# Two-layer hybrid decoder: the conditioning's slabs in the MLPs move from the weights' load places to the place of the dead normed tokens

## The chip, the cores and the metric

The kernel runs on one core of one Trainium2 chip. The metric is device time of one execution in microseconds (us). The engines are PE (TensorE, with its weight loads shown apart as PEld), DVE (VectorE), ACT (ScalarE), POOL (GpSimd) and SP (SyncE, which here only issues transfers). "The trace" is the hardware profiler's record of one execution of the kernel before.

## What is computed

Two layers of a trunk over 256 tokens of width 1024. Each layer has a part with four token mixers and an MLP. A vector c is turned by `ada_w` into six vectors per layer, the conditioning: shift, scale and gate for the mixers, and the same for the MLP.

```
c_act = silu(c)
for l in range(2):
    sh1, sc1, g1, sh2, sc2, g2 = split(c_act @ ada_w[l] + ada_b[l], 6)
    h = rmsnorm(x, norm_mix_g[l]) * (1 + sc1) + sh1
    z = h @ w_in[l]                        # 7124 columns, for the four mixers and their gates
    ... four mixers, merged by gates ...
    x = x + g1 * (merged @ w_o[l])
    h = rmsnorm(x, norm_mlp_g[l]) * (1 + sc2) + sh2
    x = x + g2 * (square(relu(h @ mlp_w1[l])) @ mlp_w2[l])
out = rmsnorm(x, final_g)
```

All of it is float32. The matrix products are made of three products of float32r parts: each weight is split into a high and a low part, and so are the tokens.

## The kernel before

**Slabs.** Every weight reaches the core as slabs of 128 partitions x 1024 float32 (512 KB; those of `w_in` may be smaller). SP loads a slab into a place named `raw`; there are five of these (`NB_RAW = 5`, pool `rawp`). ACT copies it to the high part `wh`, DVE subtracts to make the low part `wl`, and after that the place is free for the next load. `wh` and `wl` have nine places in the MLPs. PE then multiplies with both.

**The conditioning on DVE.** Ten of the twelve conditioning vectors are made on DVE (`ON_DVE`): eight slabs each of the transposed `ada_w` (`in_ada_t`). For one slab DVE multiplies it with the broadcast c (`crow`) and adds up the row, in one SCALAR_TENSOR_TENSOR that writes back into the slab's own place (`Vec.use`); nothing of it goes to ACT or PE. Those slabs sit in the same five `raw` places as the weights and are freed by that instruction. Two vectors are made at the kernel's start in places of their own (`raw0`). `PLAN` puts one in the first mixers, six in the first layer's MLP (48 slabs) and one in the second layer's MLP (8 slabs).

**The MLP.** The 4096 hidden columns are taken in 16 groups g of 256. W1 of a group is two slabs, W2 of a group two slabs. PE does W1 of groups 0 to 2 for one token half at a time, then W2 of groups 0 and 1, and from then on in turns W1(g), W2(g-1) up to W1(13), W2(12), then W1(14), W1(15), and then the rest of W2. What I call a phase below is two slabs, W1 or W2 of one group. After W1(g) ACT and POOL make the squared relu, DVE its low part `uL`, which W2(g) needs. `spread` strews the conditioning's items evenly among the items from W2(0) on.

**What sets the order.** The program is written out in one order for each engine's queue by `run()`: it walks through the items, and before an item it calls `do_split` for the slabs that the item and the next ones need (about 5500 ns ahead by the planner's own clock `Flow`), and `do_load` for the next slabs as long as a place is free in its books (`raw_free`). A load stands in SP's queue in the order of the slabs, and waits there until its place is free: SP goes on to no later load before. Likewise a SCALAR_TENSOR_TENSOR on DVE waits for its slab and holds up the `wl` behind it.

**The normed tokens.** `new_hT` makes two tiles of 128 x 8 x 256 (tags `hTh` and `hTl`, 8 KB a partition each, one buffer each, pool `actp`) for the normed tokens of the mixers. In the MLP they are dead: the MLP has its own `h2`. At the end of the first MLP they are made anew for the second layer's mixers.

Of the kernel before, what the change touches and what calls it, by code (L numbers as in the profile page):

```python
# [23 lines left out]
F32 = mybir.dt.float32  # L24
# [5 lines left out]
OP = mybir.AluOpType  # L30
# [3 lines left out]
P = 128  # L34
S = 256
NT = 2
D = 1024
KD = 8
# [21 lines left out]
PLAN = {('start', 0): ((0, 1), (0, 0)), ('mixers', 0): ((0, 3), (0, 4), (0, 2)), ('mlp', 0): ((0, 5), (1, 1), (1, 0), (1, 3), (1, 4), (1, 2)), ('mixers', 1): (), ('mlp', 1): ((1, 5),)}  # L60
ON_PE = ((0, 3), (0, 4))
ON_DVE = tuple((l, p) for l in range(2) for p in range(6) if (l, p) not in ON_PE)
# [240 lines left out]
class Slab:  # L303


    pre = use = None
    first = False

    def __init__(self, ap, shape, split=True):
        self.ap, self.shape, self.split = ap, shape, split  # L310
# [14 lines left out]
def trunk_kernel(ctx, tc, x, cT, pos, chan, ada_w, ada_t, w_in, mlp_w1, gla_gate_w,  # L325
                 gla_norm_g, hgrn_norm_g, w_branch_out, w_o, mlp_w2, final_g, out, depth=2):
    nc = tc.nc
    fl = Flow(nc)
    V, A, G, T = fl.v, fl.a, fl.g, fl.t
# [3 lines left out]
    rawp = ctx.enter_context(tc.tile_pool(name="rawp", bufs=NB_RAW))  # L333
    hlp = ctx.enter_context(tc.tile_pool(name="hlp", bufs=NB_HL))
    rows = ctx.enter_context(tc.tile_pool(name="rows", bufs=1))
    actp = ctx.enter_context(tc.tile_pool(name="actp", bufs=1))
# [41 lines left out]
    slabs = []  # L378
    pos_of = {"load": 0, "split": 0}
# [3 lines left out]
    def add(emit, need=(), before=None, cost=1300.0):  # L383
        items.append(Item(emit, need, before, cost))
        return items[-1]

    def spread(start, fill):

        main = items[start:]
        del items[start:]  # L390
        n = 0
        for i, it in enumerate(main):
            while n < len(fill) and n * len(main) < i * len(fill):
                items.append(fill[n])
                n += 1
            items.append(it)
        items.extend(fill[n:])
# [10 lines left out]
    def view(t_, shape):  # L408
        n = 1
        for d in shape[1:]:  # L410
            n *= d
        v = t_[:, :n]
        return v.rearrange("p (a b) -> p a b", b=shape[2]) if len(shape) == 3 else v

    raw_free = [0.0] * NB_RAW
    raw0 = {"free": [0.0] * NB_RAW0}
    hl_free = {"hl": [0.0] * NB_HL, "hl2": [0.0] * NB_HL2}
    sp = {"t": 0.0}

    def do_load(i):  # L420
        s = slabs[i]
        if s.pre is not None:
            s.pre()
        s.raw = view((raw0["pool"] if s.first else rawp).tile([P, 1024], F32, name="raw", tag="raw"), s.shape)
        nc.sync.dma_start(s.raw.rearrange("p a b -> p (a b)") if len(s.shape) == 3 else s.raw, s.ap)
        n = 1
        for d in s.shape:
            n *= d
        places = raw0["free"] if s.first else raw_free
        free = places.pop(0) + 60.0 if len(places) else 0.0  # L430
        sp["t"] = max(sp["t"], free) + 475.0
        start = max(fl.clock["dma"], sp["t"] + 650.0)
        fl.clock["dma"] = start + n * 4 / 360.0
        s.t_raw = fl.clock["dma"] + 908.0
        fl.arrived(s.raw, s.t_raw)

    def do_split(i, pool):
        s = slabs[i]
        if s.use is not None:
            old, fl.ctx = fl.ctx, None  # L440
            s.use()
            (raw0["free"] if s.first else raw_free).append(fl.clock["dve"])
            fl.ctx = old
        if not s.split:
            return
        s.pool = pool
        live_hl[pool] += 1
        pl = hlp if pool == "hl" else hl2["pool"]
        free = hl_free[pool].pop(hl_free[pool].index(min(hl_free[pool])))
        wh = pl.tile([P, 1024], F32R, name="wh", tag="wh")  # L450
        wl = pl.tile([P, 1024], F32R, name="wl", tag="wl")
        fl.freed(wh, free)
        fl.freed(wl, free)
        s.h, s.l = view(wh, s.shape), view(wl, s.shape)
        old, fl.ctx = fl.ctx, None
        A.activation(s.h, s.raw, AF.Copy)
        V.tensor_tensor(s.l, s.raw, s.h.bitcast(F32), op=OP.subtract)
        raw_free.append(fl.end)
        fl.ctx = old

    def run():
        order = {}
        last = {}
        for j, it in enumerate(items):
            for s in it.need:
                if id(s) not in order:
                    order[id(s)] = len(slabs)
                    slabs.append(s)
                last[id(s)] = j
        n = len(items)  # L470
        closing = [n] * (n + 1)
        for j in range(n - 1, -1, -1):
            closing[j] = j if items[j].closes else closing[j + 1]

        def room(s, j):
            go = ["hl"] if live_hl["hl"] < NB_HL else []
            if hl2["pool"] is not None and live_hl["hl2"] < NB_HL2 and last[id(s)] < closing[j]:
                go.append("hl2")
            return min(go, key=lambda p: min(hl_free[p])) if go else None

        for j, it in enumerate(items):
            if it.before is not None:
                it.before()
            must = max([order[id(s)] for s in it.need], default=-1)
            want, t, k = must, 0.0, j
            while k + 1 < n and t < (LOOK if it.look is None else it.look):
                k += 1
                want = max([want] + [order[id(s)] for s in items[k].need])
                t += items[k].cost
            while pos_of["split"] <= want:  # L490
                i = pos_of["split"]
                pool = room(slabs[i], j) if slabs[i].split else "none"
                if pool is None:
                    assert i > must, "no room for a slab"
                    break
                while pos_of["load"] < len(slabs) and (pos_of["load"] <= i or (
                        raw0["free"] if slabs[pos_of["load"]].first else raw_free)):
                    do_load(pos_of["load"])
                    pos_of["load"] += 1
                now = fl.clock["pe"]  # L500
                if i > must and (slabs[i].split or slabs[i].use) and (slabs[i].t_raw > now + EARLY or max(
                        fl.clock["dve"], fl.clock["act"]) > now + SPLIT_SLACK):
                    break
                do_split(i, pool)
                pos_of["split"] += 1
            it.emit()
            for s in it.need:
                if not s.split and s.use is None:
                    raw_free.append(fl.end)
                elif s.split and last[id(s)] == j:  # L510
                    live_hl[s.pool] -= 1
                    hl_free[s.pool].append(fl.clock["pe"] + 200.0)
            fl.weave()
# [99 lines left out]
    crow = consts.tile([P, D], F32, name="crow")  # L613
# [8 lines left out]
    class Vec:  # L622
# [5 lines left out]
            self.ready = self.summed = 0  # L628
            self.there = set()

        def fill(self, first=False):

            if (self.l, self.part) in ON_PE:
                return [it for c_ in range(2) for it in self.half(c_)]
            res = []
            for k in range(KD):
                s = Slab(ada_t[ON_DVE.index((self.l, self.part)), k], [P, D], split=False)
                s.first = first
                s.use = self.use(s, k)
                res.append(Item(lambda: None, [s], None, 0.0))  # L640
            return res
# [16 lines left out]
        def use(self, s, k):  # L658
            def f():
                if k == 0:  # L660
                    self.col = rows.tile([P, KD], F32, name="col", tag="col", bufs=8)
                V.scalar_tensor_tensor(s.raw, s.raw, 1.0, crow, op0=OP.mult, op1=OP.mult,
                                       accum_out=self.col[:, k:k + 1])
                if s.first:
                    self.summed = k + 1
                elif k == KD - 1:
                    self.finish(0, KD)
            return f

# [939 lines left out]
    vecs = {(l, p_): Vec(l, p_) for l in range(depth) for p_ in range(6)}  # L1609
    first = vecs[0, 0], vecs[0, 1]  # L1610
# [63 lines left out]
    def layer(l):  # L1674
# [18 lines left out]
        if l:  # L1693
# [10 lines left out]
            at = len(items)  # L1704
# [5 lines left out]
        else:  # L1710
# [38 lines left out]
            at = len(items)  # L1749
# [36 lines left out]
            at = len(items)  # L1786
# [175 lines left out]
        at = len(items)  # L1962
# [7 lines left out]
            if g - 1 < NG - LAG:  # L1970
                w2(g - 1)
        fill = []
        spread(at, [it for v in PLAN["mlp", l] if v[0] < depth for it in vecs[v].fill()])
        add(lambda: fl.spawn("row", gate2.to_row()), cost=0.0)

        def end(t):
# [95 lines left out]
        for t in range(NT):  # L2072
# [4 lines left out]
            for n, (c0, c1) in enumerate(ENDS[t] if l + 1 == depth else ENDS[0]):  # L2077
                for g, f_ in order[2:]:
                    part = w2_part(g, f_, s2[g][f_], t, n) if l + 1 == depth else w2_emit(g, f_, s2[g][f_], [(t, n)])
# [12 lines left out]
    for l in range(depth):  # L2092
        layer(l)
# [15 lines left out]
class _Box:  # L2109

    v = None
# [65 lines left out]
```

## Time and profile before

| | us |
|---|---|
| median of 3 runs | 925.19 |
| lowest, highest | 925.08, 925.54 |
| the profiled execution | 929.37 |
| its span in the trace | 927.6 |
| PE busy in the span | 893.1 |
| DVE, ACT, POOL busy | 718.7, 496.6, 102.0 |

The trace comes from the profiled execution, which took 4.2 us more than the median; durations below are from it. The first layer's MLP lies at about 287 to 490 us of the span, the second's at about 736 us to the end. A busy PE in such a table is a modelled busy time: whether PE is held up inside it is read from the distance between the starts of its matmuls.

### The profile page before, as it was taken

The page shows a single profiled execution, that of the slowest core. Times are in us where ns is not written, and L with a number is a line of the kernel's source. Part 1 is how long each engine was busy: PE and PEld are TensorE (multiplying, and loading weights), DVE is VectorE, ACT ScalarE, POOL GpSimd, SP SyncE. Part 2 cuts the span into 40 slices and gives each one's busy share as a digit, 9 for nine tenths or more (in the row PEclk, how much of TensorE's full clock was granted, in tenths as well). Part 3 has the DMA queues.
Part 4 walks back from the last instruction along what each step waited for, and adds up shares of the span by engine and source line. Part 5 has one row for each costly group of instructions (what it writes and reads, how often), then busy time and mean ns, then how long its engine had stood idle before and what let it go on. Part 6 is the DMA issues. An engine that isn't in the chain of part 4 may idle for free.

```text
span 927.6 us, 13933 instructions
## 1 busy us (share of the span) xinstructions
PE 893.1 (96%) x5092; PEld 744.7 (80%) x5092; DVE 718.7 (77%) x1230; ACT 496.6 (54%) x845; POOL 102.0 (11%) x146
## 2 busy tenths in 40 slices
PE   6999999999999999989899999999999999999997
PEld 6986677677788998878878987777887888888885
DVE  6969888897678887788876987889667785666664
ACT  6775843445456444434465668544455465555552
POOL 3051010201000011101120000100200001111110
PEclk9999999999999999999999999999999999999999
DMA  9965554667654898988854554535454546656651
GB/s 367 379 227 167 182 185 156 186 224 245 207 181 137 301 325 326 320 305 316 319 193 152 180 159 140 175 100 160 163 189 149 177 163 220 228 204 209 220 184 46
DMA packets 55557, 196.41 MB, mean 212 GB/s; under 512 B 6432, under 2 KB 7104, under 8 KB 55488
## 3 DMA queue, kind: packets, MB, share of 16 engines
q1 hardware_dynamic: 54768, 194.98, 61.4%
q8 instruction: 40, 0.66, 0.3%
q10 hardware_dynamic: 720, 0.54, 0.2%
q14 instruction: 29, 0.24, 0.1%
HBM read 194.44 MB, written 1.05 MB: 211 GB/s over the span
## 4 chain that ended last, share of the span: by engine, by line
PE 65%; issue 16%; DVE 13%; ACT 3%; POOL 2%; DMA 2%; POOLq 0%; DVEq 0%; ACTq 0%
PE mm L281 44%; PE acc L281 14%; PE b L281 6%; DVE wl L281 4%; DVE raw L281 2%; DVE uL L281 1%; PE accs L281 1%; DMA raw<-in_mlp_w 1%; ACT wh L281 1%; DVE gate L281 1%; DVE ca L281 1%; DVE sc L281 0%; DMA ccol<-in_cT 0%; DVE hTl L281 0%; DVE x L281 0%
## 5 line engine op out<-in xcount | busy, mean ns | idle before, releaser
L281 DVE TENSOR_TENSOR wl<-raw,wh 128x1024 fp32r<-128x1024 f32 (+1 forms) x276 | 327.7, 1215 | 71.6 <-ACT wh L281 70.0
L281 ACT ACTIVATE wh<-raw 128x1024 fp32r<-128x1024 f32 (+1 forms) x276 | 277.6, 1042 | 129.6 <-DMA raw<-in_mlp_w 88.8
L281 PE MATMUL mm<-wh,hTh 128*128 128x512 f32 (+1 forms) x384 | 155.7, 406 | 3.9 <-ACT hTh L281 2.5
L281 PE MATMUL mm<-wh,hTl 128*128 128x512 f32 (+1 forms) x384 | 148.2, 386 | 0.8 <-DVE hTl L281 0.8
L281 PE MATMUL mm<-h,wh 128*128 128x256 f32 (+1 forms) x624 | 148.1, 318 | 0.0
L281 PE MATMUL mm<-wl,hTh 128*128 128x512 f32 (+1 forms) x384 | 147.6, 384 | 0.0
L281 PE MATMUL mm<-h,wl 128*128 128x256 f32 x416 | 117.9, 283 | 3.0 <-DVE wl L281 3.0
L281 PEld LDWEIGHTS mm<-h,wh 128*128 128x128 f32 x624 | 103.8, 188 | 9.9
L281 PE MATMUL acc<-wl,uH 128*128 128x512 f32 (+1 forms) x256 | 101.1, 395 | 4.8 <-DVE wl L281 4.8
L281 PE MATMUL acc<-wh,uL 128*128 128x512 f32 (+1 forms) x256 | 100.7, 393 | 1.2 <-DVE uL L281 1.2
L281 PE MATMUL acc<-wh,uH 128*128 128x512 f32 (+1 forms) x256 | 101.6, 397 | 0.0
L281 PEld LDWEIGHTS mm<-wh,hTh 128*128 128x128 f32 x384 | 73.5, 191 | 29.7 <-issue 7.8
L281 DVE SCALAR_TENSOR_TENSOR raw<-raw,crow 128x1024 f32<-128x1024 f32 x80 | 96.8, 1217 | 0.3 <-DMA raw<-in_ada_t 0.2
L281 PEld LDWEIGHTS mm<-wh,hTl 128*128 128x128 f32 x384 | 73.3, 191 | 15.4 <-DVE hTl L281 1.9
L281 PEld LDWEIGHTS mm<-h,wl 128*128 128x128 f32 x416 | 78.3, 188 | 5.0 <-DVE wl L281 4.2
L281 PEld LDWEIGHTS mm<-wl,hTh 128*128 128x128 f32 x384 | 73.6, 192 | 10.2
L281 PEld LDWEIGHTS acc<-wl,uH 128*128 128x128 f32 x256 | 48.2, 188 | 16.6 <-DVE wl L281 6.8
L281 DVE SCALAR_TENSOR_TENSOR ca<-U,chp,ca 128x256 f32<-128x256 f32 x120 | 58.4, 502 | 0.0
L281 PEld LDWEIGHTS acc<-wh,uL 128*128 128x128 f32 x256 | 48.1, 188 | 12.6 <-DVE uL L281 1.7
L281 PEld LDWEIGHTS acc<-wh,uH 128*128 128x128 f32 x256 | 48.2, 188 | 10.2
L281 PE MATMUL mm<-wh,h 128*128 128x256 f32 x192 | 36.6, 286 | 0.0
L281 ACT ACTIVATE junk<-x 128x512 bf16<-128x512 f32 (+2 forms) x19 | 12.4, 654 | 42.8 <-DVE x L281 42.8
(605 smaller groups left out, 1395.4 us busy)
## 6 DMA issues: line engine op xcount, KB each, us to landing
raw<-in_mlp_w SPq DMA_DIRECT2D x128, 512.0 KB, 4.9
raw<-in_w_in SPq DMA_DIRECT2D x100, 512.0 KB, 3.9
raw<-in_ada_t SPq DMA_DIRECT2D x80, 512.0 KB, 5.1
raw<-in_ada_w SPq DMA_DIRECT2D x16, 512.0 KB, 3.9
raw<-in_w_branch_out SPq DMA_DIRECT2D x16, 512.0 KB, 4.1
raw<-in_w_o SPq DMA_DIRECT2D x16, 512.0 KB, 4.7
raw<-in_w_in SPq DMA_DIRECT2D x16, 362.0 KB, 6.2
x<-in_x SPq DMA_DIRECT2D x2, 512.0 KB, 4.4
```

What stands on the lines that cost most here:

```text
L281: return fn(*args, **kw)
```

## The change

In the MLPs a conditioning slab is loaded together with the next one: one transfer of 128 x 2 x 1024 (1 MB), into a tile `rawa` that takes the place (the tag) of `hTl` and `hTh` in turns. Such a double has its own list of two places (`rawm`), and the weights keep all five `raw` places. `Vec.use` runs its DVE instruction for both halves, one right after the other. In the first MLP 48 loads become 24, in the second 8 become 4. The instructions on DVE, ACT, POOL and PE stay the same in number. The start and the mixers are as before.

```diff
+    rawm = {"free": [0.0] * 2, "n": 0}
...
+    def places_of(s):
+
+        return raw0["free"] if s.first else rawm["free"] if s.mlp else raw_free
+
+    def raw_tile(s):
+        if s.mlp:
+            rawm["n"] += 1
+            return actp.tile([P, 2 * D], F32, name="rawa", tag="hT" + "hl"[rawm["n"] % 2])
+        return (raw0["pool"] if s.first else rawp).tile([P, 1024], F32, name="raw", tag="raw")
...
-        s.raw = view((raw0["pool"] if s.first else rawp).tile([P, 1024], F32, name="raw", tag="raw"), s.shape)
-        nc.sync.dma_start(s.raw.rearrange("p a b -> p (a b)") if len(s.shape) == 3 else s.raw, s.ap)
+        s.raw = view(raw_tile(s), s.shape)
+        nc.sync.dma_start(s.raw.rearrange("p a b -> p (a b)") if len(s.shape) == 3 and not s.mlp else s.raw, s.ap)
...
-                while pos_of["load"] < len(slabs) and (pos_of["load"] <= i or (
-                        raw0["free"] if slabs[pos_of["load"]].first else raw_free)):
+                while pos_of["load"] < len(slabs) and (
+                        pos_of["load"] <= i or places_of(slabs[pos_of["load"]])):
...
-            for k in range(KD):
-                s = Slab(ada_t[ON_DVE.index((self.l, self.part)), k], [P, D], split=False)
-                s.first = first
+            part = ada_t[ON_DVE.index((self.l, self.part))]
+            for k in range(0, KD, 2 if mlp else 1):
+                if mlp:
+                    s = Slab(part[k:k + 2].rearrange("a p d -> p a d"), [P, 2, D], split=False)
+                else:
+                    s = Slab(part[k], [P, D], split=False)
+                s.first, s.mlp = first, mlp
...
-                V.scalar_tensor_tensor(s.raw, s.raw, 1.0, crow, op0=OP.mult, op1=OP.mult,
-                                       accum_out=self.col[:, k:k + 1])
+                for a in range(2 if s.mlp else 1):
+                    r_ = s.raw[:, a, :] if s.mlp else s.raw
+                    V.scalar_tensor_tensor(r_, r_, 1.0, crow, op0=OP.mult, op1=OP.mult,
+                                           accum_out=self.col[:, k + a:k + a + 1])
```

How the instructions move, at two places of the first MLP, both in its steady part; the numbers in a name only tell tiles apart.

SP's queue before, the loads around W2(5) (`raw_3516`, `raw_3553`) and W1(7) (`raw_3587`, `raw_3608`):

```order
L425 DMA raw_3513<-in_ada_t 128x1024
L425 DMA raw_3516<-in_mlp_w2 128x1024
L425 DMA raw_3548<-in_ada_t 128x1024
L425 DMA raw_3553<-in_mlp_w2 128x1024
L425 DMA raw_3583<-in_ada_t 128x1024
L425 DMA raw_3587<-in_mlp_w1 128x1024
L425 DMA raw_3605<-in_ada_t 128x1024
L425 DMA raw_3608<-in_mlp_w1 128x1024
```

All eight take one of the same five places in turn. SP's queue now, the same weights (`raw_3453`, `raw_3471`, `raw_3509`, `raw_3541`):

```order
L437 DMA rawa_3451<-in_ada_t 128x2x1024
L437 DMA raw_3453<-in_mlp_w2 128x1024
L437 DMA raw_3471<-in_mlp_w2 128x1024
L437 DMA rawa_3507<-in_ada_t 128x2x1024
L437 DMA raw_3509<-in_mlp_w1 128x1024
L437 DMA raw_3541<-in_mlp_w1 128x1024
```

Six transfers of the same bytes; a double stands ahead of each two weights, and each double waits for the double two before it.

DVE's queue before, the same four weights:

```order
L281 SCALAR_TENSOR_TENSOR raw_3513,col_3585<-raw_3513,crow_97 128x1024
L281 TENSOR_TENSOR wl_3590<-raw_3516,wh_3589 128x1024
L281 SCALAR_TENSOR_TENSOR raw_3548,col_3585<-raw_3548,crow_97 128x1024
L281 TENSOR_TENSOR wl_3611<-raw_3553,wh_3610 128x1024
L281 SCALAR_TENSOR_TENSOR raw_3583,col_3585<-raw_3583,crow_97 128x1024
L281 TENSOR_TENSOR wl_3646<-raw_3587,wh_3645 128x1024
L281 SCALAR_TENSOR_TENSOR raw_3605,col_3585<-raw_3605,crow_97 128x1024
L281 TENSOR_TENSOR wl_3681<-raw_3608,wh_3680 128x1024
L281 TENSOR_TENSOR uL_3674<-u__3687,uH_3673 128x256
L281 TENSOR_TENSOR uL_3674<-u__3688,uH_3673 128x256
```

A conditioning slab and a weight take turns, and `uL` follows after four of each. DVE's queue now:

```order
L281 SCALAR_TENSOR_TENSOR rawa_3451,col_3571<-rawa_3451,crow_97 128x1024 x2
L281 TENSOR_TENSOR wl_3579<-raw_3453,wh_3578 128x1024
L281 TENSOR_TENSOR wl_3597<-raw_3471,wh_3596 128x1024
L281 SCALAR_TENSOR_TENSOR rawa_3507,col_3571<-rawa_3507,crow_97 128x1024 x2
L281 TENSOR_TENSOR wl_3633<-raw_3509,wh_3632 128x1024
L281 TENSOR_TENSOR wl_3665<-raw_3541,wh_3664 128x1024
L281 TENSOR_TENSOR uL_3661<-u__3671,uH_3660 128x256
L281 TENSOR_TENSOR uL_3661<-u__3672,uH_3660 128x256
```

The two conditioning instructions now stand together ahead of two weights, and `uL` stands behind the same four weights. On PE only a few transposes at the first MLP's and the second MLP's beginning move by three to fifteen matmuls; on ACT a few copies of slabs move past each other there; POOL's order is the same.

## Rows read from the trace of the kernel before

**Rows 1.** The page: busy us and share; GB/s of transfers in 40 slices.
```profile
PE 893.1 (96%) x5092; PEld 744.7 (80%) x5092; DVE 718.7 (77%) x1230; ACT 496.6 (54%) x845; POOL 102.0 (11%) x146
GB/s 367 379 227 167 182 185 156 186 224 245 207 181 137 301 325 326 320 305 316 319 193 152 180 159 140 175 100 160 163 189 149 177 163 220 228 204 209 220 184 46
```

**Rows 2.** Stretches: length, busy PE, PEld, DVE, ACT, POOL, clock, DMA share, GB/s.
```profile
319.11:364.28 45.17, 45.17 (x289) 40.84 (x288) 37.40 (x51) 18.71 (x27) 5.87 (x6) 1.00 0.92 328
364.28:466.19 101.91, 94.07 (x602) 83.42 (x600) 81.69 (x112) 44.64 (x66) 15.65 (x16) 1.00 0.90 317
768.21:902.14 133.93, 133.93 (x681) 113.38 (x680) 83.16 (x111) 73.53 (x122) 16.67 (x24) 1.00 0.61 212
```

**Rows 3.** PE in order of time: start, us, matmul, [idle before <-releaser].
```profile
370.15 0.39 PE L281 MATMUL acc<-wh,uH 128*128 128x512 f32 x1
371.35 0.51 PE L281 MATMUL acc<-wl,uH 128*128 128x512 f32 x1 [0.81 <-DVE wl L281]
```

**Rows 4.** Who waited for whom, 307 to 467: total us, times, longest.
```profile
ACT wh L281 <- DMA raw<-in_mlp_w: 84.7, 48, 4.2
DVE wl L281 <- ACT wh L281: 23.1, 24, 2.2
...
PE acc L281 <- DVE wl L281: 4.8, 6, 1.1
...
PE mm L281 <- DVE wl L281: 3.0, 5, 0.9
```

**Rows 5.** What SP's queue waited for, 307 to 467.
```profile
SPq L425 <- DVE wl L281: 62.5, 50, 2.4
SPq L425 <- DVE raw L281: 49.2, 41, 2.5
```

**Rows 6.** The load line, 364 to 466: issue ns min/median/max; time to landing.
```profile
L425 SPq DMA_DIRECT2D raw<-in_mlp_w x35: 327/328/636, 365.0 to 464.2; - x35
...
L425 SPq DMA_DIRECT2D raw<-in_ada_t x27: 327/328/328, 363.8 to 452.9; - x27
...
DMA to landing us min/median/max: 3.6/5.2/6.3
```

**Rows 7.** DVE in order of time.
```profile
406.24 0.82 DVE L281 TENSOR_TENSOR uL<-u__4058,uH 128x256 fp32r<-128x256 f32 x1 [0.51 <-POOL u__4058 L281]
...
407.32 1.21 DVE L281 SCALAR_TENSOR_TENSOR raw<-raw,crow 128x1024 f32<-128x1024 f32 x1
...
409.83 1.22 DVE L281 SCALAR_TENSOR_TENSOR raw<-raw,crow 128x1024 f32<-128x1024 f32 x1
...
410.97 1.22 DVE L281 TENSOR_TENSOR wl<-raw,wh 128x1024 fp32r<-128x1024 f32 x1
```

**Rows 8.** Groups by line, 303 to 467: busy us, mean ns; idle before.
```profile
L281 ACT ACTIVATE wh<-raw 128x1024 fp32r<-128x1024 f32 x54 | 57.3, 1062 | 89.3 <-DMA raw<-in_mlp_w 84.7 <-DVE uL L281 2.6 <-DVE wl L281 2.0
```

**Rows 9.** Stretches as in Rows 2, start and MLP.
```profile
5.00:42.00 37.00, 33.50 (x214) 32.08 (x214) 33.50 (x81) 26.74 (x49) 6.38 (x29) 0.95 1.03 411
...
320.00:330.00 10.00, 10.00 (x65) 8.99 (x65) 8.10 (x11) 4.71 (x8) 1.41 (x2) 1.00 0.99 365
```

**Rows 10.** Transfers issued in 5 to 42: count, size, median us to landing.
```profile
raw<-in_ada_t SPq DMA_DIRECT2D x14, 512.0 KB, 7.7
```

**Rows 11.** PE in order of time, end of the first MLP.
```profile
474.33 0.50 PE L281 MATMUL acc<-wh,uL 128*128 128x512 f32 x1 [1.24 <-DVE uL L281]
```

**Rows 12.** ACT in order of time, there.
```profile
465.72 1.06 ACT L281 ACTIVATE wh<-raw 128x1024 fp32r<-128x1024 f32 x1 [0.64 <-DMA raw<-in_mlp_w]
466.68 0.36 ACT L281 ACTIVATE r__4688<-mm 128x256 f32<-128x256 f32 x1
```

**Rows 13.** PE's matmuls with `hTl`, 240 to 300: count, ns, first and last start.
```profile
L281 PE MATMUL mm<-wh,hTl x16: 388/389/398, 240.1 to 259.7; 128*128 128x512 f32 x16
```

**Rows 14.** SP's queue in order of time: start, us.
```profile
286.42 0.33 SPq L425 DMA_DIRECT2D raw<-in_ada_t  x1
...
302.58 0.33 SPq L425 DMA_DIRECT2D raw<-in_ada_t  x1
```

More of the change, by code (lines that the diff above doesn't have):

```diff
@@ L306 @@
     pre = use = None
-    first = False
+    first = mlp = False
     def __init__(self, ap, shape, split=True):
@@ L428, in do_load @@
             n *= d
-        places = raw0["free"] if s.first else raw_free
+        places = places_of(s)
         free = places.pop(0) + 60.0 if len(places) else 0.0
@@ L441, in do_split @@
             s.use()
-            (raw0["free"] if s.first else raw_free).append(fl.clock["dve"])
+            places_of(s).append(fl.clock["dve"])
             fl.ctx = old
@@ L629, in __init__, with fill @@
             self.there = set()
-        def fill(self, first=False):
+        def fill(self, first=False, mlp=False):
             if (self.l, self.part) in ON_PE:
@@ L661, in f @@
                     self.col = rows.tile([P, KD], F32, name="col", tag="col", bufs=8)
-                V.scalar_tensor_tensor(s.raw, s.raw, 1.0, crow, op0=OP.mult, op1=OP.mult,
-                                       accum_out=self.col[:, k:k + 1])
+                for a in range(2 if s.mlp else 1):
+                    r_ = s.raw[:, a, :] if s.mlp else s.raw
+                    V.scalar_tensor_tensor(r_, r_, 1.0, crow, op0=OP.mult, op1=OP.mult,
+                                           accum_out=self.col[:, k + a:k + a + 1])
                 if s.first:
                     self.summed = k + 1
-                elif k == KD - 1:
+                elif k + a == KD - 1:
                     self.finish(0, KD)
@@ L1972, in layer @@
         fill = []
-        spread(at, [it for v in PLAN["mlp", l] if v[0] < depth for it in vecs[v].fill()])
+        spread(at, [it for v in PLAN["mlp", l] if v[0] < depth
+                    for it in vecs[v].fill(mlp=True)])
         add(lambda: fl.spawn("row", gate2.to_row()), cost=0.0)
```

## The prediction, made before the changed kernel ran

> **What bounds the kernel now.** I read the page first: PE is busy for 893.1 of 927.6 us, so time can be won only where PE stands still or is slowed, and the slices of transfer rate are level at 305 to 326 GB/s for the length of the first MLP, far above the stages beside it [rows 1]. Then the stretches: from 319.11 to 364.28 PE does four phases of W1 and four of W2 in 45.17 us, 5.65 us each; from 364.28 to 466.19 it does nine and seven, 16 phases, in 101.91 us, 6.37 us each [rows 2]. At the earlier pace these would take 16 x 5.65 = 90.3 us. So 11.6 us are lost there. The view of waits names less, 4.8 + 3.0 us [rows 4], because a wait costs more than its idle time: where 0.81 us of idle are shown, the matmul starts 1.20 us after the one before it [rows 3], and matmuls in a row stand 0.23 us apart.
>
> What PE waits for is `wl` on DVE. DVE waits for `wh` on ACT (23.1 us), and ACT for the weights' transfers: 84.7 us in 48 waits, in 54 copies of slabs [rows 4, 8]. At the transfers the chain does not end: SP waits too, 62.5 us for `wl` and 49.2 us for the conditioning's instruction, that is for a free place [rows 5]. It is a ring. From 364 to 466 SP issued 35 + 27 = 62 loads [rows 6], one in 1.64 us, so each of the five places comes round in 8.2 us. Its parts: issue 0.33 and landing 5.2 [rows 6], ACT 1.06 [rows 8], DVE's step 1.14 (the distance of two starts) [rows 7], together 7.7, and some hops between engines. 524 KB in 1.64 us are the 317 GB/s of this stretch. That the transfer engines can do more shows at 320 to 330, 365 GB/s with the same kind of slabs, and at the kernel's start, 411 GB/s for 37 us with 13 places [rows 9].
>
> The second MLP has one conditioning slab to some seven weights and the same ring: PE is busy for all of 133.93 us [rows 2]. Nothing can be won there by earlier weights.
>
> **The change, part by part.**
>
> More room in the first MLP. The ring of five now serves weights alone, two in a phase of 5.65 us. At a cycle of 8.2 us five places could give 3.4 weights in a phase; that ring no longer binds. The doubles have two places, one double in a phase, so each has 2 x 5.65 = 11.3 us for its round: issue 0.33, landing, and two DVE steps of 1.14 [rows 7]. That leaves 8.7 us for landing. The trace has no 1 MB transfer. Lower bound: 5.2 us [rows 6] and the second half's bytes at 411 GB/s, 1.3 us, 6.5 us. Upper bound: the 7.7 us of a 512 KB slab at the start, with more in flight [rows 10], and 1.4 us at 365 GB/s, 9.1 us. I take 6.7, near the lower one, since the landing of 5.2 us is from this stage. At 9.1 us a round takes 11.7 us, a phase 5.85, and over some 22 steady phases 4 us would be lost. In SP's queue the weights stand behind a double that waits for its place; the weights behind it are needed two doubles later, about 11 us, so they have the same slack as it.
>
> What is late next? Transfers: a group of two phases with four weights and two doubles moves 8 x 0.524 = 4.19 MB. At 411 GB/s this takes 10.2 us, at 365 GB/s 11.5 us, PE takes 11.3. There are six such groups in a row at most (the others have one double), so at 365 GB/s 6 x 0.2 = 1.2 us are lost, at 411 nothing; I charge 0.6. DVE: 8 steps of 1.14, the `uL` pair 1.08 (406.24 to 407.32) and its wait for POOL of 0.5 [rows 7] make 10.7 us of 11.3. DVE stays the faster one, by 5%.
>
> The Trainium skill speaks against this part: "DMA: Bandwidth & Descriptors", section "Specifications", gives about 358 GB/s as a core's limit from HBM. By it the group would take 11.7 us, an estimate, and six groups would lose 2.5 us instead of 0.6. The 411 GB/s of [rows 9] are above that limit, so I keep to the rows.
>
> The start of the stage. Before, SP gets to the first conditioning slab at 286.42, and then has its places full until 302.58, while DVE is busy with the norms [rows 14]. Now the two doubles and two or three weights more are under way in that time, about three slabs of lead. PE does not wait there, so this is worth nothing by itself; it is cover for the point above. The first double waits for PE's last matmul with `hTl`, which started at 259.7 [rows 13], 27 us earlier: no wait. At the end, the second layer's normed tokens need the tiles only after the last double is read, some 20 us before: nothing.
>
> Pairs on DVE. A `wl` may stand behind two conditioning instructions instead of one, 1.14 us later, and every second one stands behind none. `uL` stands behind the same weights as before. While weights come early this is covered by DVE's lead, several us of it; without that cover it would cost up to 1.1 us in 24 places, 27 us, and at the least nothing, or a small gain where the weight is the late one. I take nothing, as the lead decides.
>
> 28 loads fewer: at 0.33 us each 9 us of SP's queue, which waits most of the time: nothing. A double's issue may take longer than 0.33, covered likewise. PE's moved transposes: nothing.
>
> The tail of the first MLP. At 474.33 PE waited 1.24 us for `uL` [rows 11]. ACT's relu of that chain was at 466.68, behind a copy that had waited 0.64 us for its slab [rows 12]; with slabs early the relu runs when PE is done with W1. I count 1.2 us. Bounds: 0, if POOL and DVE are what is late, and 1.2.
>
> **The sum.** 11.6 + 1.2 - 0.6 = 12.2 us won. The profiled execution took 929.37 us, so it would take 917.2; it stands 4.2 us above the median, 925.19, for which I predict **913.0 us**. What follows the first MLP moves forward as a whole: the slabs of `w_in` use the weights' five places as before.
>
> **Rivals.**
>
> 1. *Only the bound moves, and most of the gain stays away.* DVE with 10.7 of 11.3 us, or the doubles' landing at 9.1 us, takes over. For it: DVE's margin is only 0.6 us a group, and one wait for ACT or POOL a group more eats it. Against: 319 to 364, where PE ran unslowed with the same DVE work. If each of the nine groups of 364 to 466 loses half a microsecond to a whole one, 4.5 to 9 us go, and the time is 917 to 922.
>
> 2. *Slower: the ring of two.* In-order queues make a double that lands late hold up DVE and, on SP, the weights. Two places bind harder than the five did if a round exceeds 2 x 6.37 = 12.7 us, that is if landing exceeds 12.7 - 2.6 = 10.1 us. Against: my upper bound is 9.1. For it: 9 slabs can now be under way, 4.7 MB, which at 365 GB/s take 13 us if all are queued at once. At a landing of 11 us a phase takes 6.8 us; 24 of them lose 0.43 us each against today, some 10 us: 935.
>
> 3. *No change.* The 317 GB/s are what the memory gives in this stage, places or not, and the doubles only queue longer: 925. For it: the share of busy transfer engines is already 0.90 [rows 2]. Against: 365 GB/s in the same stage [rows 9]. That the change does not do what it says belongs here; the order of the queues shows that it does.
>
> **How the numbers follow.** Forecast (10 to 14 us won, 911 to 915) 0.70; rival 1 0.16; rival 2 0.06; rival 3 0.08. The range: no lower than 15 us won, as 12.8 is all that was found and matmuls at their best in that stage would give some two more: 910. Upwards it takes in half of rival 1: 919.5. Faster by over 0.2% (1.9 us, about what a measurement of this kernel can tell from no change): 0.70 + 0.16 = 0.86. Within it: 0.07. Slower: 0.07, rival 2 and a rest of rival 3.
>
> **What would show it.** Right: the 16 phases that took 101.91 us take about 91, no `wl` waits of PE in the first MLP, transfers there at 340 GB/s or more, ACT's wait for `mlp_w` well under 84.7 us, SP's loads of weights issued earlier before their use, the second MLP as before. Wrong: phases still over 6 us. Then either DVE has no idle time left (rival 1), or DVE waits for a double with landings near 10 us (rival 2), or landings grew with the rate still at 317 (rival 3).

## The result and the profile after

| | us |
|---|---|
| kernel after, median of 4 (lowest, highest) | 911.66 (910.59, 916.08) |
| kernel before beside it, median of 4 (lowest, highest) | 925.13 (923.6, 925.54) |
| ratio, 95% interval | 0.9866 (0.9831 to 0.9902) |
| predicted | 913.0 (910.0 to 919.5) |
| profiled execution after, its span | 912.58, 910.8 |

The change wins 13.5 us, 925.13 - 911.66 (9.1 to 15.6 by the interval); the forecast was 12.2. It lies where the forecast put it.

The page of the kernel after: busy us and share of each engine; GB/s in 40 slices.

```profile
PE 885.3 (97%) x5092; PEld 741.0 (81%) x5092; DVE 713.2 (78%) x1230; ACT 497.4 (55%) x845; POOL 98.3 (11%) x146
GB/s 365 393 218 175 189 161 168 183 211 254 236 201 196 230 386 376 375 380 307 277 118 169 149 152 155 170 116 165 137 185 197 195 165 206 242 194 235 191 155 48
```

Beside [rows 1]: the level 305 to 326 GB/s of the first MLP has become 375 to 386 GB/s, and then it falls off sooner (307, 277, 118), because the same bytes have been moved.

Stretches of the kernel after (us, busy PE, PEld, DVE, ACT, POOL, clock, share of DMA, GB/s): the opening of the first MLP, its first eight phases, its next 16 phases, and 135 us of the second MLP:

```profile
307.27:318.88 11.61, 11.61 (x55) 9.38 (x53) 11.61 (x18) 4.55 (x7) 0.00 (x0) 1.00 0.99 379
318.88:364.12 45.24, 45.24 (x289) 40.91 (x288) 41.38 (x61) 22.70 (x33) 7.45 (x8) 1.00 0.99 381
364.12:454.41 90.29, 90.29 (x602) 82.78 (x600) 78.02 (x108) 45.83 (x67) 14.31 (x17) 1.00 0.89 338
750.00:885.00 135.00, 135.00 (x685) 114.17 (x684) 82.70 (x109) 72.82 (x122) 16.63 (x24) 1.00 0.60 210
```

The 16 phases that took 101.91 us in [rows 2] take 90.29 us, with PE busy in all of it. The forecast had 90.3.

Waits of the kernel after, all of PE's from 290 to 480 us; then one row each of ACT's and DVE's and two of SP's queue from 307 to 456 us (total us, times, longest):

```profile
PE mm L281 <- DVE u__2993 L281: 0.9, 1, 0.9
```
```profile
ACT wh L281 <- DMA raw<-in_mlp_w: 37.8, 30, 4.2
```
```profile
DVE uL L281 <- ACT uH L281: 14.9, 12, 3.2
```
```profile
SPq L437 <- DVE rawa L281: 51.9, 16, 4.7
SPq L437 <- DVE wl L281: 38.5, 39, 5.4
```

PE's waits for `wl` of [rows 4] are gone. ACT's wait for the weights fell from 84.7 to 37.8 us. DVE now waits 14.9 us for `uH`, which ACT makes of PE's result; before, no such wait stood among DVE's. I read this as the chain having turned round: the weights' parts are ready before PE needs them.

**Where the time went in the two traces.** The spans are 16.8 us apart, 3.3 us more than the medians. I compared the starts of the same matmuls. From before to after the shift is -0.2 us up to 319 us, then -11.6 over the 16 phases, -0.3 behind them, and -1.4 where PE had waited 1.24 us for `uL` [rows 11]: -13.5 us together (the one at 474.33 now starts at 460.83). Of the other 3.3 us, 1.5 and 1.6 us lie at two places behind the first MLP and are not the change's. The kernel before there, then the same places of the kernel after (columns as above):

```profile
498.00:505.00 7.00, 6.51 (x29) 6.35 (x30) 2.71 (x8) 2.80 (x9) 0.15 (x1) 0.76 0.00 0
700.00:705.00 5.00, 5.00 (x21) 4.05 (x20) 3.03 (x5) 0.60 (x1) 0.00 (x0) 0.66 0.34 102
```
```profile
485.00:491.00 6.00, 6.00 (x36) 5.84 (x37) 2.54 (x8) 3.31 (x8) 0.15 (x1) 1.00 0.00 0
685.00:690.00 5.00, 5.00 (x28) 4.11 (x27) 3.89 (x7) 2.32 (x4) 0.00 (x0) 1.00 0.27 104
```

The column to read is the clock, 0.76 and 0.66 against 1.00: in that one execution of the kernel before PE ran for a part of both stretches at the lower of its two levels. A second profile of the unchanged kernel after has it too (below), so an execution of either kernel may show it. This is why the medians, and not the spans, give the gain.

### The profile page after: what moved, and what is told of

Read it like the earlier page. It is cut to its first block, busy times and chain, and to the rows that moved or that the text cites. A ratio compares the mean times of both kernels' runs of the same rounds, so it can differ in the third digit from the quotient of the medians.

```text
span 910.8 us, 13891 instructions
## 1 busy us (share of the span) xinstructions
PE 885.3 (97%) x5092; PEld 741.0 (81%) x5092; DVE 713.2 (78%) x1230; ACT 497.4 (55%) x845; POOL 98.3 (11%) x146
## 4 chain that ended last, share of the span: by engine, by line
PE 83%; DVE 10%; issue 3%; ACT 2%; DMA 0%; POOL 0%; POOLq 0%; DVEq 0%; ACTq 0%
PE mm L281 53%; PE acc L281 23%; PE b L281 6%; DVE wl L281 4%; PE accs L281 1%; DVE raw L281 1%; DVE gate L281 1%; ACT wh L281 1%; DVE ca L281 1%; DVE sc L281 0%; DMA ccol<-in_cT 0%; DVE hTl L281 0%; DVE x L281 0%; DVE tm L281 0%; DVE ynorm L281 0%
## 5 line engine op out<-in xcount | busy, mean ns | idle before, releaser
L281 DVE SCALAR_TENSOR_TENSOR rawa<-rawa,crow 128x1024 f32<-128x1024 f32 x56 | 66.1, 1217 | 0.2 <-DMA rawa<-in_ada_t 0.2
L281 PEld LDWEIGHTS acc<-wh,uL 128*128 128x128 f32 x256 | 48.1, 188 | 11.3
```

The costliest lines, as they stand in the source:

```text
L281: return fn(*args, **kw)
```

## Experiments

The theory: one round of a place (issue, landing, ACT's copy, DVE's step), divided by five places, is the interval of the loads; PE needs them faster, and the change wins because more bytes have places at once. Rivals: the 1 MB transfers are what is faster; the order of loads in pairs is; the weights must have places without the conditioning's slabs between them; or DVE, close to its limit, would have taken the gain. Ratios are against the kernel before on the same chip.

| kernel | us, median (lowest, highest) | ratio (95%) | the 16 phases |
|---|---|---|---|
| before, first set / second set / last set | 925.92 / 924.65 / 924.22 | 1 | 101.91 |
| after, again | 911.39 (910.68, 915.83) | 0.9855 (0.9822 to 0.9888) | 90.29 |
| before, six places, planner told | 918.98 (918.76, 919.4) | 0.9928 (0.9905 to 0.995) | 90.29 |
| before, a sixth place, same order | 912.77 (910.83, 915.03) | 0.987 (0.9835 to 0.9905) | 90.29 |
| before, loads in pairs, five places | 926.21 (922.6, 928.69) | 1.0009 (0.9987 to 1.0031) | 102.55 |
| after, doubles as two loads | 912.35 (912.13, 914.45) | 0.9855 (0.9828 to 0.9881) | 90.29 |
| after, one slab in each of the two places | 926.14 (922.19, 927.58) | 1.0017 (0.9995 to 1.0039) | 102.92 |
| after, one double place | 944.14 (942.62, 945.66) | 1.0219 (1.0192 to 1.0247) | 112.15 |
| after, extra DVE steps | 929.7 (927.23, 930.88) | 1.0059 (1.0039 to 1.008) | 101.78 |
| after, first MLP alone | 913.04 (912.33, 914.2) | 0.9886 (0.9868 to 0.9903) | 90.29 |
| after, six places, planner told | 918.15 (914.11, 919.99) | 0.9912 (0.9878 to 0.9947) | 90.29 |
| after, a sixth place, same order | 912.3 (912.12, 915.18) | 0.9871 (0.9837 to 0.9905) | 90.28 |

**The kernel after, unchanged, once more.**

> The changed kernel once more, on the same chip as the three beside it, to have its spread there. Every theory: 910.5 to 916 us, the 16 phases at the end of the first MLP in about 90.3 us. The upper part of that range would come with stretches at the lower granted clock, not with waits.

911.39 us. Its profiled execution has a span of 914.1 us, 3.3 us longer than the first profile's, and 3.1 us of that lie at the two places named above (1.5 and 1.6 us); the same windows of it:

```profile
485.00:491.00 6.00, 5.90 (x26) 5.74 (x27) 2.46 (x8) 1.84 (x7) 0.15 (x1) 0.72 0.00 0
685.00:690.00 5.00, 4.45 (x14) 3.54 (x15) 3.26 (x5) 0.00 (x0) 0.00 (x0) 0.68 0.30 105
```

So the kernel's own spread of some 3 us in these two profiles is the clock at these places, whatever the first MLP does.

**Is it the number of places?** One more shared place, and nothing else of the change: single loads of 512 KB, kinds mixed as before.

```diff
-NB_RAW = 5
+NB_RAW = 6
```

> The kernel before with six shared places for slabs instead of five; conditioning slabs stay single and share them. Theory (the ring of places sets the rate): a place's round of 8.2 us over six places is 1.37 us a slab, against 1.46 us that PE needs on average (62 slabs in 90.3 us); but landings grow with the rate (5.2 us before, 7.6 us in the changed kernel), so the round grows to some 9 us, 1.5 us a slab. The 16 phases fall from 101.9 us to 90 to 95 us, and the time to 912 to 919 us. Rival (what counts is the 1 MB transfers, or that the two kinds of slabs have places apart): 922 to 926 us, phases at 99 us or more.

The 16 phases take 90.29 us, as in the kernel after; the whole kernel is only 6.9 us faster than before (925.92 - 918.98). The planner's books know `NB_RAW`, so it wrote the mixers in another order too, and these lost 2.8 us by the start of the 16 phases. Most of the rest lies at the two places of the clock, where it fell in this trace too: matmul for matmul this trace ends 10.8 us ahead of that of the kernel before, which had the same two falls. This run mixed two things, so the place was added behind the planner's back:

```diff
-    rawp = ctx.enter_context(tc.tile_pool(name="rawp", bufs=NB_RAW))
+    rawp = ctx.enter_context(tc.tile_pool(name="rawp", bufs=NB_RAW + 1))
```

> The kernel before, every engine's instructions in exactly its order, with one place more in the pool of slabs: the planner still counts five, so only the tile that a load waits for is one slab older. Theory (ring of places): the 16 phases at the end of the first MLP take about 90.3 us instead of 101.9, the tail's wait for the low part of u (1.2 us) goes too, and the mixers, whose order was moved in the run with six planned places, do not lose: 910 to 914 us. Rival (the win of that stage needs the slabs of the conditioning apart from the weights, or the other order): 917 us or more.

Every engine's instructions stand in the order of the kernel before. 912.77 us: the whole gain of the change. Its 16 phases, and its load line there:

```profile
362.04:452.33 90.29, 90.29 (x601) 82.78 (x600) 81.92 (x111) 46.68 (x68) 16.40 (x17) 1.00 0.96 359
```
```profile
L425 SPq DMA_DIRECT2D raw<-in_mlp_w x33: 327/328/611, 362.6 to 443.9; - x33
L425 SPq DMA_DIRECT2D raw<-in_ada_t x24: 327/328/328, 364.9 to 433.2; - x24
...
DMA to landing us min/median/max: 3.5/5.8/7.8
```

A slab lands 0.6 us later than with five places (5.8 against 5.2 [rows 6]), so the round of 8.2 us becomes 8.8, an estimate, and six places give a load each 1.47 us. The 62 loads of [rows 6], spread over 90.29 us, would be one each 1.46 us. By this the ring is just wide enough. In the trace it is a little faster: these 57 loads went out one in 1.45 us, the last 8.4 us before the end of the phases (443.9 to 452.33; before, 464.2 to 466.19), so PE is the bound. 0.5 MB of room did what the change does with 2 MB of dead tiles. That the weights must be apart from the conditioning falls as a cause.

**Is it the transfer's size?** Each double filled by two transfers of 512 KB:

```diff
+        if s.mlp:
+            for a_ in range(2):
+                nc.sync.dma_start(s.raw[:, a_, :], s.ap[:, a_, :])
...
```

> The changed kernel, but each double is filled by two transfers of 512 KB, one behind the other on the queue, instead of one of 1 MB. Places and the order of all engines as in the changed kernel. Theory (places): no difference to the changed kernel, within 2 us of it, 16 phases in 90.3 us. Rival (the larger transfer is what wins): back towards the kernel before, 918 us or more, with PE waiting for low parts of weights again.

912.35 us and 90.29 us for the 16 phases: size decides nothing here. The first eight phases moved 381 GB/s, as with transfers of 1 MB:

```profile
319.25:364.41 45.16, 45.16 (x289) 40.84 (x288) 41.58 (x61) 22.77 (x33) 7.31 (x8) 1.00 0.99 381
```

The Trainium skill ("DMA: Bandwidth & Descriptors", "Rules for kernel authors") advises 1 MiB and more per transfer for the highest rate; between 512 KB and 1 MB this kernel, with several transfers under way at once, shows no difference that can be told from none.

**Is it the order?** The kernel before with the conditioning's slabs in pairs, so that the queues have the order A A W W (A the conditioning, W weights), in the five places:

```diff
-                res.append(Item(lambda: None, [s], None, 0.0))
+                if mlp and k % 2:
+                    res[-1].need.append(s)
+                else:
+                    res.append(Item(lambda: None, [s], None, 0.0))
...
```

> The kernel before with only the order of the changed one: two slabs of the conditioning, then two weights, all single transfers in the five shared places. Theory (places): the round of five is what it was, 100 to 106 us for the 16 phases, 923 to 931 us. Rival (the win is the order, fewer turns between the two kinds on DVE and SP): 911 to 918 us.

926.21 us, phases 102.55 us, and PE's waits for `wl` stay (290 to 480 us):

```profile
PE mm L281 <- DVE wl L281: 5.1, 6, 1.8
PE acc L281 <- DVE wl L281: 2.3, 5, 0.6
```

The order by itself wins nothing.

**How much room must the two places have?** One slab of 512 KB in each of the two tags, single loads:

```diff
-            return actp.tile([P, 2 * D], F32, name="rawa", tag="hT" + "hl"[rawm["n"] % 2])
+            return actp.tile([P, D], F32, name="rawa", tag="hT" + "hl"[rawm["n"] % 2])
...
```

> The changed kernel with one slab of the conditioning in each of the two places (512 KB transfers, one slab at a time): seven places in all, more than the five before, but two of them for the conditioning. Theory (ring for each kind): a round of 0.33 + 5 to 7 + 1.14 us and hops, 7 to 9 us, over two places is 3.5 to 4.5 us a slab where PE's pace needs one in 3.0 us; the 16 phases, with some 30 conditioning slabs, take 105 to 130 us, the whole stage loses more than before: 930 to 965 us. Rival (any room beyond five helps): 911 to 920 us.

926.14 us: the whole gain is gone, though there are seven places of 512 KB, one more than in the kernel before with a sixth. What SP's queue waited for from 307 to 467 us; four of its loads in order (start us, us); and all loads of A in the 16 phases (count, issue ns, first and last start):

```profile
SPq L437 <- DVE rawa L281: 100.9, 42, 5.8
...
SPq L437 <- DVE wl L281: 5.5, 4, 2.4
```
```profile
393.51 0.33 SPq L437 DMA_DIRECT2D rawa<-in_ada_t  x1
393.93 0.38 SPq L437 DMA_DIRECT2D raw<-in_mlp_w  x1
397.05 0.33 SPq L437 DMA_DIRECT2D rawa<-in_ada_t  x1
397.47 0.38 SPq L437 DMA_DIRECT2D raw<-in_mlp_w  x1
```
```profile
L437 SPq DMA_DIRECT2D rawa<-in_ada_t x27: 327/328/328, 367.5 to 455.8; - x27
```

SP stands almost all its waiting time before a load of A; the weights' five places are seldom what it waits for. A W follows 0.4 us behind an A. The 27 loads of A come one in 3.40 us, a round of 6.8 us over the two places; in the kernel before they came one in 3.43 us (363.8 to 452.9 [rows 6]), and with a sixth shared place one in 2.97. So seven places bring the conditioning no faster than five shared ones, and the 16 phases take as long. I had expected worse (a round of 7 to 9 us, 105 to 130 us for the phases, 930 to 965 us), because I took a longer landing than the 4.2 us (median of A) that came. That the queues tie the weights to the ring of A is what these rows suggest; it was not tried by itself.

**One place for the doubles instead of two.**

```diff
-    rawm = {"free": [0.0] * 2, "n": 0}
+    rawm = {"free": [0.0] * 1, "n": 0}
...
-            return actp.tile([P, 2 * D], F32, name="rawa", tag="hT" + "hl"[rawm["n"] % 2])
+            return actp.tile([P, 2 * D], F32, name="rawa", tag="hTl")
```

> The kernel after with one place for the doubles instead of two. Theory (the ring of places sets the rate): a single place's round is its issue of 0.38 us, a landing of 4 to 6 us, two adds of 1.14 us and the hops, so some 7.5 to 8.6 us for a double, where a phase is 5.65 us. Once the lead is used up, each of the last phases is as long as that round: the 16 phases take 118 to 135 us instead of 90.3, and the kernel 940 to 970 us. Rival (the doubles' landing is not on the path, only that the weights have five places to themselves counts): the 16 phases stay at 90 to 95 us and the kernel at 912 to 918 us.

944.14 us (two executions), inside the expectation, and 112.15 us for the 16 phases, a little under it. The stretch (columns as for the stretches), three loads of SP's queue in it, and DVE's wait for A in it:

```profile
372.32:484.47 112.15, 98.75 (x601) 85.78 (x601) 83.73 (x114) 46.81 (x68) 14.97 (x16) 0.97 0.79 297
```
```profile
372.40 0.38 SPq L437 DMA_DIRECT2D rawa<-in_ada_t  x1
...
379.76 0.38 SPq L437 DMA_DIRECT2D rawa<-in_ada_t  x1
...
470.27 0.38 SPq L437 DMA_DIRECT2D rawa<-in_ada_t  x1
```
```profile
DVE rawa L281 <- DMA rawa<-in_ada_t: 23.5, 14, 3.0
```

From 372.40 to 470.27 there are 13 rounds, 7.53 us each, where a phase at PE's pace is 5.65 us: 97.87 of the 112.15 us. The rest is behind the last issue. The parts of one round: from 379.76 to landing 4.74 us, the two steps on DVE 2.39, some hops, and at 387.00 the next issue. The granted clock was 0.97 in this stretch, so a part of the loss may be the clock's. This is the mechanism of rival 2, with one place: the ring of A is slower than PE and sets the pace, for the weights behind it too.

**Has DVE room?** One more multiply of a whole slab for each double, into the half that is dead by then:

```diff
+                if s.mlp:
+                    nc.vector.tensor_tensor(s.raw[:, 1, :], s.raw[:, 1, :], crow, op=OP.mult)
```

> The kernel after with one more VectorE multiply of a whole slab for each double, into the half of the place that is already dead; what is stored is unchanged. Theory (VectorE has a small margin: 119.4 us busy of the 135.5 us from 318.88 to 454.41 us): some 20 extra steps of 1.14 us in that stretch are 23 us of work for 16 us of room, so VectorE becomes what sets the end, and the kernel takes 918 to 926 us; TensorE then waits for wl in the last phases. Rival (VectorE has ample room, since it waits for others): 911 to 914 us, no waits of TensorE in the first MLP.

929.7 us, 18 us above the kernel after and above what I expected. DVE in the 16 phases (columns as for the stretches), the extra steps, and PE's waits from 318 to 475 us; last, the kernel after from the eight phases' start to the end of the 16:

```profile
368.22:470.00 101.78, 93.55 (x601) 83.06 (x600) 101.27 (x127) 44.38 (x67) 21.44 (x16) 1.00 0.84 309
```
```profile
L683 DVE TENSOR_TENSOR rawa<-rawa,crow x24: 1224/1226/1511, 306.7 to 461.9; 128x1024 f32<-128x1024 f32 x24
```
```profile
PE mm L281 <- DVE wl L281: 5.2, 7, 0.8
PE acc L281 <- DVE wl L281: 4.2, 7, 0.7
```
```profile
318.88:454.41 135.53, 135.53 (x890) 123.70 (x888) 119.40 (x168) 68.53 (x100) 21.75 (x25) 1.00 0.92 352
```

DVE is busy for 101.27 of 101.78 us, and PE waits for `wl` again. The extra steps are 24 x 1.15 (the distance of two starts, 400.83 to 401.98), 27.6 us; the end of the 16 phases moved 15.6 us (454.41 to 470.00). So DVE took up some 12 us of them, not the 16.1 (135.53 - 119.40) that I read from its idle time. A part of the idle time seems to stand where it cannot be filled, as where DVE waits for what PE makes; that was not shown by itself. The rest up to 18 us came later, some of it with the clock at 0.72 from 700 to 706. The kernel after is thus some 12 us of DVE work away from rival 1.

**Is any of it in the second MLP?** Doubles in the first MLP alone:

```diff
-                    for it in vecs[v].fill(mlp=True)])
+                    for it in vecs[v].fill(mlp=l == 0)])
```

> The kernel after with the doubles in the first MLP alone; the second MLP loads the conditioning's slabs one at a time into the five shared places, as before. Theory (the whole win is in the 16 phases of the first MLP; the second has a margin of loads): 911 to 914 us, the 16 phases at 90.3 us, the second MLP's stretch as long as in the kernel after within 0.5 us. Rival (a part of the win lies in the second MLP or the tail's place): 916 to 924 us.

913.04 us, the span 910.9 against 910.8 us, and PE busy in all of the second MLP's 135 us as in the kernel after:

```profile
750.00:885.00 135.00, 135.00 (x685) 114.17 (x685) 83.81 (x110) 73.59 (x123) 16.64 (x24) 1.00 0.61 214
```

Nothing of the gain is there.

**Would more room win more?** The kernel after with a sixth place, once told to the planner (`NB_RAW = 6`), once not (`bufs=NB_RAW + 1`).

> The changed kernel with six places for weights instead of five, as a candidate for a faster version. Theory: the first MLP has no wait for weights left, so six places win nothing there; other stages with weights may win a little or nothing: 909 to 913 us, within 2 us of the changed kernel. Rival (weights' places still bind somewhere): 4 us or more faster.

> The changed kernel, order unchanged, with one more place for weights in the pool. Theory: no weight is late in the first MLP, so nothing is won there; the small waits for weights in the mixers (some 4 us in the kernel before) may shrink: 908 to 912 us. Rival (six places do harm by themselves, as the run with six planned places could be read): 915 us or more.

918.15 us and 912.3 us. The first missed: the phases are at 90.29 us, but with the planner's other order some 4 us are lost in the first mixers by 266 us, one more fall of the clock among them (0.89 granted from 190 to 205 us, 1.00 in the kernel after). The second came out 0.3 us above its range, and the 16 phases take 90.28 us: there is nothing left to win in the MLP. No kernel tried beats the kernel after by what can be measured; the kernel before with a sixth place equals it with one constant.

## Why the prediction was right, step by step

- **The loss of 11.6 us and its cause.** Right in size (101.91 to 90.29) and in cause. The round of five places as the limit is shown by the sixth place alone (90.29), by the one double place (a slower ring, rounds of 7.53 us, slower phases), and by what did not matter: size and order. One part was put down wrongly: ACT's 1.06 us stands in the round of the 35 weights only, not in that of the 27 conditioning slabs, so the parts come to 7.3 us on the mean, and 0.9 of the 8.2 us are hops and queues, not 0.5. The Trainium skill ("Perfetto Trace Analysis", "Optimization Strategy") reads a gap that comes back on the engine that should be full as a possible sign of too little room for the next tile; PE's eleven waits for `wl` [rows 4] and the sixth place agree.
- **Landing of the doubles.** Taken at 6.7 us, bounds 6.5 to 9.1, limit 8.7. From 300 to 460 us it was:

```profile
DMA to landing us min/median/max: 4.9/7.4/9.6
```

  So the median was above what I took, and single ones were above both my upper bound and the limit. PE lost nothing to them (busy for 45.24 of 45.24 and 90.29 of 90.29 us), and DVE waited for a double once, for 0.2 us. The issue took 0.38 us instead of 0.33. The weights, too, landed later than I had reckoned: I left their ring at the old round of 8.2 us, but at 8.7 us landing in the first eight phases (last section) the round is some 11.7 us (8.2 - 5.2 + 8.7), an estimate, and five places give 2.4 weights in a phase, not 3.4. That is still above the two that PE needs; the sum came out, but with less to spare than it said.
- **The charge for the rate, 0.6 us.** It did not come: 381 GB/s in the first eight phases, and PE at 5.65 us a phase. By my estimate from the figure of the Trainium skill ("DMA: Bandwidth & Descriptors", "Specifications", about 358 GB/s) 2.5 us should have gone; the 381 GB/s are above that figure, and the measurement decides.
- **The tail, 1.2 us.** It gave 1.4 us: no wait for `uL` is left among PE's waits.
- **The sum.** 13.5 us instead of 12.2. The differences are the charge that did not come (0.6), the tail (0.2), and 0.2 and 0.3 us before and behind the 16 phases that I had not seen. Taking the gain off the median came out: the shifts apart from the two places of the clock are 13.5 us, as the medians' difference is. The profiled execution had some 3.1 us of the clock at those places; how much of its 4.2 us above the median that explains is open, since the median's execution left no trace.
- **Rival 1, DVE.** I saw 10.7 of 11.3 us a group. In the opening DVE is full, 11.61 of 11.61 us; in the eight phases it is busy for 41.38 of 45.24; in the 16 phases for 78.02 of 90.29. It did not take over. In the eight phases it is busy for 10.3 us a group (two phases), in the 16 for 9.8, so the margin was larger than the 5% that I gave it. The rival's price was reckoned with nine groups; 16 phases are eight groups, 4 to 8 us.
- **Rival 2, the ring of two.** It did not decide with 1 MB in each place, but its mechanism is real: with one place the kernel is 2.2% slower than before, and with 512 KB in each of two all of the gain is gone. Its price was set too low: of the 24 phases only 16 took 6.37 us, the other eight took 5.65, so phases of 6.8 us would have cost some 16 us, not 10.
- **Rival 3, the memory's rate.** Ruled out: the 317 GB/s of [rows 2] were the ring's, with one place more the same stage moves 359.
- **What was to be seen.** Transfers at 340 GB/s or more: 338 over the 16 phases, just short of it, and 381 before them, since the loads run ahead (the last weight of this MLP was issued at 445.4 us instead of 464.2 [rows 6]). The other marks came as written.

## What to carry to other kernels

Where loads share a few places, work out the round of a place (issue, landing, all that reads it, hops) and divide by the number of places: if that is longer than the time in which the consumer uses one, the transfers' rate is the ring's and not the memory's, as it was here, and one place more may do all that there is to do. Count it for each ring by itself: where the queue waited 100.9 us for the places of A and 5.5 us for those of W, loads whose places were free stood behind the one that had none. And where a planner knows the number of places, add the place also without telling it, or the new order hides what the place is worth.

## What the runs showed of the hardware

- The landing time depends on the load: 5.2 us at 317 GB/s [rows 2, 6], 5.8 at 359 with six places, and in the first eight phases of the kernel after, at 381 GB/s (its load line, both kinds):

```profile
DMA to landing us min/median/max: 6.6/8.4/10.2
```
```profile
raw<-in_mlp_w SPq DMA_DIRECT2D x17, 512.0 KB, 8.7
rawa<-in_ada_t SPq DMA_DIRECT2D x8, 1024.0 KB, 8.3
```

  The two rows below it are the medians of each kind. The sixth place and the doubles give the same 90.29 us, so here, with PE as the bound, more in flight only landed later. A round worked out with the landing time of the slower kernel is too short.
- A transfer of 1 MB landed in 4.9 us (median of the kernel with one double place, where the 16 phases moved 297 GB/s on the mean), less than the 5.2 us of 512 KB slabs in the kernel before. In that run the 512 KB weights, issued right behind a double, landed in 6.3 us (median): what is already under way seems to count for more than the size.
- After PE had stood idle for a moment at the start of the second mixers, the granted clock fell in some executions and not in others of the same kernel. The matmuls of the kernel before there, still at the lower level (1.2 GHz) and then at the upper (2.4 GHz):

```profile
501.53 0.50 PE L281 MATMUL mm<-wl,hTh 128*128 128x362 f32 x1
501.83 0.50 PE L281 MATMUL mm<-wh,hTl 128*128 128x362 f32 x1
...
502.54 0.33 PE L281 MATMUL mm<-wh,hTl 128*128 128x362 f32 x1
502.71 0.33 PE L281 MATMUL mm<-wh,hTh 128*128 128x362 f32 x1
```

  0.30 us apart, then 0.17. It cost 1.5 us there, and 1.6 us at the second place. In the 3 us ahead PE was busy for 1.65 us in the kernel before. At the same place of the kernel after it was busy for 1.20 us in the first profile, where the clock did not fall, and for 1.19 us in the second, where it fell:

```profile
495.00:498.00 3.00, 1.65 (x12) 1.12 (x10) 1.10 (x3) 1.45 (x7) 0.54 (x1) 1.00 0.40 157
```
```profile
482.00:485.00 3.00, 1.20 (x9) 0.96 (x9) 1.30 (x4) 1.89 (x7) 0.43 (x1) 1.00 0.43 172
```
```profile
482.20:485.20 3.00, 1.19 (x9) 0.96 (x9) 1.30 (x4) 1.89 (x7) 0.44 (x1) 1.00 0.18 70
```

  So PE's work there does not tell which execution it strikes; what does stays open.
